# Small loads and norm roots issued earlier, and one placement for every buffer of weight parts, in a two-block transformer kernel

## The chip, the cores and the metric

The kernel runs on one core of a Trainium2 chip. The time is the device time of one execution in microseconds (us), and less is better. PE is the matrix engine, DVE the vector engine, ACT the scalar engine, POOL GpSimd, and SP the engine that issues the weight loads.

## The reference, cut to what matters

Two transformer blocks act on x of 256 tokens by 1024, in float32. The first is a hybrid mixer (a convolution of 31 taps beside an attention over selected blocks), a cross-attention to 256 memory rows, and a SwiGLU layer, followed by a norm. The second is a gated and a dilated branch beside each other, and a layer of 16384 experts.

```python
for l in range(DEPTH):                       # first block
    h = rms_norm(x, norm_mix_g[l])
    x = x + hybrid_mixer(h, w_in[l], conv_dw_w[l], ...)   # w_u ... w_gates, conv_pw_w, w_out
    h = rms_norm(x, norm_x_g[l])
    x = x + cross_attention(h, mem, xq_w[l], xkv_w[l], xo_w[l])
    h = rms_norm(x, norm_ffn_g[l])
    x = x + swiglu(h, ffn_in_w[l], ffn_out_w[l])
x = rms_norm(x, final_norm_g)
h = rms_norm_2(x, norm1_g[layer])            # second block; two norms stand in a row here
proj = h @ w_in[layer]                       # w_uv_2, w_qkv_2
...
x = x + mix @ w_out[layer]                   # w_out_2
x = x + peer(rms_norm_2(x, norm2_g[layer]), w_query[layer], sub_keys[layer], expert_u[layer], expert_v[layer])
```

## The kernel before, in words

**Products in three parts.** A float32 product is made from parts: a weight is cast to a shorter float (hi), the rest is a second one (lo), and the activations are held as hi and lo as well (hh and hl). A product is hi·hh + hi·hl + lo·hh. `form2` (L273) holds the weight still and streams 256 tokens past it: a unit of half a chunk is 24 matmuls. `form1` (L283 to L285) holds the activations still and streams 512 weight columns.

**The stream of weights.** `Stream` loads chunks of 1 MB through SP into three raw buffers, in the order of use. Each chunk is two units. ACT casts a unit to hi (L100), DVE subtracts to lo (L111); hi and lo go into pairs of buffers used in turn, four of them at first, six where `add_pairs` has added hi_x and lo_x. In pair 0 the parts of some weights (the tuple `moved`) begin 40 elements further on. DVE's subtraction frees the raw buffer, and so lets SP issue the next chunk. ACT and DVE take their work strictly in the order of the program: a part that stands behind a waiting instruction waits too.

**Late work.** `defer` and `pending` hold an evacuation back until some matmuls of the next unit stand ahead of it (`run_late`); `bg` is a list of pieces that `run_bg` spreads over the units of a product. `cols2` makes two units and one evacuation, `rows_c` (a product with its result in rows of tokens) ends in `tail`.

**A tail.** `tail` makes the last four chunks of a product in four groups (two halves of tokens, tt, by two of columns, hf), evacuates each (adds the residual, multiplies with the gain of the next norm), squares on ACT, and turns the result with PE (`transpose_split`, L394 or L396) into hh (ACT cast, L400) and hl (DVE, L401), the inputs of the next product. The factor of the norm, 1/root of the mean square, is found per token: an addition on DVE, a power on POOL (L440, L477), then a multiplication into a unit matrix on DVE (`diag`, L442, L483) which PE turns into a row (L484). `scaled_norm` applies the row at the evacuation of the next product, so that the product itself can start without it. `root` calls it from the tail, where the diagonal takes part in the turn.

**Five places.** The change touches the following, in the order of time. Place 0: the convolution's taps (`cacc`, a first tap on ACT at L573, the rest on DVE at L576), which run beside the product w_u. They need the taps' weights `dww` and `cvec`, loaded by POOL at L553 and L556, behind the loads that lay out the position bias: brow is copied to `b_dram` in eight pieces (L544) and read back in two (L547). Place A: the tail of conv_pw_w. Place B: the tail of w_out, with the products xq_w and xkv_k behind it. Place C: the tail of xo_w, with ffn_in_w behind it. Place D: the tail of ffn_out_w, where `after4` makes both norms that stand in a row, with w_uv_2 behind it. Place E: the tail of w_out_2, with w_query_2 behind it.

```python
        st.split(st.n_used + st.ahead)      # tail, before: all splits that have a buffer
        st.flush()
        if after is not None:               # the roots stand behind them
            after(0)
            after(1)
```

## Time and profile before

| what | value |
|---|---|
| median of 3 runs | 1567.42 us (1566.62 to 1567.6) |
| the profiled execution | 1564.88 us, span 1563.1 us |
| PE busy | 1498.3 us, 96% of the span, 9934 matmuls |
| DVE busy | 1124.2 us, 72% |
| ACT busy | 825.9 us, 53% |
| POOL busy | 45.0 us, 3% |
| granted clock, mean | 0.986 |

The span is the time from the first to the last instruction of the trace. The profiled execution is 1.78 us longer than its span and 2.5 us shorter than the median. A busy share is a mean over all stages of the kernel. A granted clock of 1.00 is full speed (2.4 GHz), 0.50 is the lower of the two levels (1.2 GHz).

### The profile page before, as it was taken

What the parts mean: (1) busy time and instruction counts of PE and PEld (TensorE: products, weight loads), DVE (VectorE), ACT (ScalarE), POOL (GpSimd) and SP (SyncE); (2) the same over time, 40 slices, a digit from 0 to 9 for tenths busy, and PEclk for the clock granted to TensorE, in tenths of its full rate; (3) what the DMA queues carried; (4) which work ended last, traced back from release to release, by engine and by line L of the source; (5) the groups of instructions that cost most, each with busy time, mean ns of one, the idle gap of its engine ahead of it and who ended that gap; (6) DMA issues with size and microseconds to landing.
All of it is one profiled execution on the core that took longest, in us unless ns stands there. A gap on an engine that the chain in (4) does not pass through costs nothing.

```text
span 1563.1 us, 25016 instructions
## 1 busy us (share of the span) xinstructions
PE 1498.3 (96%) x9934; PEld 1357.6 (87%) x9934; DVE 1124.2 (72%) x2081; ACT 825.9 (53%) x1316; POOL 45.0 (3%) x86
## 2 busy tenths in 40 slices
PE   7699999997999999799999999999999999999998
PEld 7699788777889988587999999999999888888886
DVE  5597899665567755575889978999996555555555
ACT  5343576744455543564554557776655444444443
POOL 2210000000000000200000000000000000000000
PEclk9899999998999999899999999999999999999999
DMA  8655222454355554541545553343335655555552
GB/s 293 217 202 181 82 82 101 147 197 167 117 189 189 194 210 140 205 156 73 196 166 186 188 190 135 138 156 139 136 136 216 238 202 192 189 191 192 200 197 81
DMA packets 39733, 265.99 MB, mean 170 GB/s; under 512 B 4768, under 2 KB 5072, under 8 KB 9536
## 3 DMA queue, kind: packets, MB, share of 16 engines
q1 hardware_dynamic: 34992, 248.72, 44.1%
q0 software_dynamic: 3616, 12.53, 2.6%
q10 hardware_dynamic: 1008, 3.15, 0.6%
q8 instruction: 78, 1.28, 0.3%
q14 instruction: 39, 0.32, 0.1%
HBM read 258.09 MB, written 5.24 MB: 168 GB/s over the span
## 4 chain that ended last, share of the span: by engine, by line
PE 87%; DVE 5%; DMA 3%; ACT 2%; issue 1%; POOL 1%; SPq 0%; POOLq 0%; ACTq 0%; DVEq 0%
PE mm L273 36%; PE mm L285 12%; PE mm L284 12%; PE mm L283 12%; PE tp L1481 4%; DVE lo L111 2%; PE tp L263 2%; PE tp L273 2%; DMA b_dram<-brow 1%; DVE cacc L576 1%; PE tp L794 1%; PE pv L829 1%; DMA gain<-in_norm_mix_g_dram 1%; PE tp L816 1%; PE tp L394 0%
## 5 line engine op out<-in xcount | busy, mean ns | idle before, releaser
L100 ACT CAST hi<-raw 128x1024 fp32r<-128x1024 f32 x427 | 446.0, 1049 | 441.5 <-PE mm L285 220.8
L111 DVE TENSOR_TENSOR lo<-raw,hi 128x1024 fp32r<-128x1024 f32 x427 | 516.7, 1221 | 91.9 <-ACT hi L100 91.4
L273 PE MATMUL mm<-xnt,hi 128*128 128x256 f32 x2416 | 425.4, 280 | 8.6 <-ACT hi L100 8.6
L273 PEld LDWEIGHTS mm<-xnt,hi 128*128 128x128 f32 x2416 | 367.9, 189 | 9.2 <-ACT hi L100 8.6
L273 PE MATMUL mm<-xnt,lo 128*128 128x256 f32 x1208 | 336.4, 278 | 0.5 <-DVE lo L111 0.5
L273 PEld LDWEIGHTS mm<-xnt,lo 128*128 128x128 f32 x1208 | 228.5, 189 | 0.8 <-DVE lo L111 0.8
L283 PE MATMUL mm<-hi,wring 128*128 128x512 f32 x512 | 199.3, 389 | 1.2 <-ACT wring L256 1.2
L284 PE MATMUL mm<-lo,wring 128*128 128x512 f32 x512 | 199.3, 389 | 0.1
L285 PE MATMUL mm<-hi,wring 128*128 128x512 f32 x512 | 199.3, 389 | 0.1
L273 PE MATMUL mm<-hh,hi 128*128 128x256 f32 x976 | 172.0, 280 | 3.2 <-DVE hh L401 2.4
L273 PEld LDWEIGHTS mm<-hh,hi 128*128 128x128 f32 x976 | 149.7, 190 | 4.9 <-DVE hh L401 3.0
L273 PE MATMUL mm<-hh,lo 128*128 128x256 f32 x488 | 136.8, 280 | 15.2 <-DVE lo L111 15.2
L257 DVE TENSOR_TENSOR wring<-act,wring 128x512 fp32r<-128x512 f32 x64 | 44.2, 694 | 123.9 <-ACT wring L256 123.9
L283 PEld LDWEIGHTS mm<-hi,wring 128*128 128x128 f32 x512 | 96.1, 188 | 21.4 <-ACT wring L256 1.4
L285 PEld LDWEIGHTS mm<-hi,wring 128*128 128x128 f32 x512 | 96.1, 188 | 20.5 <-DVE wring L257 0.5
L284 PEld LDWEIGHTS mm<-lo,wring 128*128 128x128 f32 x512 | 96.1, 188 | 20.3 <-DVE lo L111 0.6
L576 DVE SCALAR_TENSOR_TENSOR cacc<-vpad,dww,cacc 128x256 f32<-128x256 f32 x240 | 101.0, 485 | 16.4 <-ACT cacc L573 16.4
L273 PEld LDWEIGHTS mm<-hh,lo 128*128 128x128 f32 x488 | 93.1, 191 | 15.6 <-DVE lo L111 15.6
L1487 DVE TENSOR_TENSOR act<-act,tp 128x208 f32<-128x208 f32 (+31 forms) x64 | 57.4, 915 | 10.6 <-PE tp L1481 8.3
L100 ACT CAST hi_x<-raw 128x1024 fp32r<-128x1024 f32 x40 | 41.9, 1051 | 38.6 <-PE mm L273 16.0
L1481 PE MATMUL tp<-raw 128*128 128x128 f32 x512 | 62.2, 275 | 0.0
L1481 PEld LDWEIGHTS tp<-raw 128*128 128x128 f32 x512 | 59.7, 191 | 0.0
(401 smaller groups left out, 2204.8 us busy)
## 6 DMA issues: line engine op xcount, KB each, us to landing
raw<-in_expert_u_dram SPq DMA_DIRECT2D x64, 1024.0 KB, 4.8
raw<-in_expert_v_dram SPq DMA_DIRECT2D x64, 1024.0 KB, 4.8
raw<-in_ffn_in_w_dram SPq DMA_DIRECT2D x22, 1024.0 KB, 4.8
raw<-in_ffn_out_w_dram SPq DMA_DIRECT2D x11, 1024.0 KB, 4.8
raw<-in_w_u_dram SPq DMA_DIRECT2D x8, 1024.0 KB, 8.7
raw<-in_w_g_dram SPq DMA_DIRECT2D x8, 1024.0 KB, 4.8
raw<-in_w_out_dram SPq DMA_DIRECT2D x8, 1024.0 KB, 4.8
raw<-in_w_query_dram SPq DMA_DIRECT2D x8, 1024.0 KB, 5.4
```

Of the source, the lines that this page charges most:

```text
L100: self.nc.scalar.copy(out=hi, in_=raw)
L111: self.nc.vector.tensor_tensor(out=lo, in0=raw, in1=hi.bitcast(F32), op=ALU.subtract)
L257: V.tensor_tensor(out=lo, in0=src, in1=hi.bitcast(F32), op=ALU.subtract)
L263: T.matmul(out=ps, lhsT=a, rhs=b, start=(k == 0), stop=(k == n - 1))
L273: T.matmul(out=ps, lhsT=a[:, k, :], rhs=b[:, k, :], start=k == 0 and n == 0, stop=k == KK - 1 and n == 2)
L283: T.matmul(out=ps, lhsT=a, rhs=r, start=first and k == 0, stop=False)
L284: T.matmul(out=ps, lhsT=a, rhs=q, start=False, stop=False)
L285: T.matmul(out=ps, lhsT=b, rhs=r, start=False, stop=last and k == nk - 1)
L576: V.scalar_tensor_tensor(out=cacc[:, j, :], in0=vpad[:, j, w:w + S], scalar=dww[:, j, w:w + 1], in1=cacc[:, j, :], op0=ALU.mult, op1=ALU.add)
L794: T.matmul(out=sv, lhsT=qT[:, (g // 2) * 4 + r, tt * P:(tt + 1) * P], rhs=ksw[:, g // 2, g % 2, :, 0:n], start=True, stop=True)
L1481: T.matmul(out=ps[:, j * P:(j + 1) * P], lhsT=ring[:, b % 2, 0, j, :], rhs=ring[:, b % 2, 1, j, :], start=True, stop=True)
L1487: V.tensor_tensor(out=o[:, :, 0:there], in0=o[:, :, 0:there], in1=pv[:, :, 0:there], op=ALU.mult)
```

## The change

The loads of small tables at place 0 move ahead of the position bias, and are issued by POOL right behind the first norm's powers. In `tail` the splits that were made at the end move behind the roots, and the units' last split in the middle goes; with a `root` all four groups are now made before the turns. `scaled_norm` makes both diagonals in `after`, right behind the roots, and the row only when an evacuation asks for it. The products of xkv_k that stood between w_out's tail and its last turn come half before it and half behind it. The first products of ffn_in_w and w_query_2 are made in halves: the first four row blocks of both units, then the last four, so that the second half of hh and hl is wanted later. The last turn of conv_pw_w's result is held back into w_out (`hold`), and in `rows_c` run at the third unit. `after4` is gone: its squares, multiplications and roots are spread over the units of w_uv_2 through `bg`, and the first block's final gain is loaded anew by POOL, 512 KB in broadcast, into the tile `ug`, behind the eight loads of that stage. All four pairs of buffers now have one size and begin at one position, and w_v, xkv_v and w_g begin 48 elements further on in every pair. Small spacing tiles, one buffer of `sn` and the place of `skT` follow from that.

```diff
-    def __init__(self, nc, raws, pairs, chunks, plain, ahead, moved):
+    def __init__(self, nc, raws, pairs, chunks, plain, gap, behind):
...
-                at = self.at if pair is self.wide and name in self.moved else 0
+                at = self.gap if name in self.behind else 0
...
-    his, los = ([const.tile([P, HF + 64], F32R, name=f"{n}0")] + fixed(const, 3, F32R, n + "_") for n in ("hi", "lo"))
+    his, los = ([const.tile([P, HF + 64], F32R, name=f"{n}{k}") for k in range(4)] for n in ("hi", "lo"))
...
-    st = Stream(nc, raws, list(zip(his, los)), chunks, ("mem", "cmp_w1"), AHEAD,
-                ("xkv_k", "w_u", "w_k", "w_c", "w_q", "w_gates", "xq_w", "ffn_in_w", "w_query_2", "expert_u_2"))
+    st = Stream(nc, raws, list(zip(his, los)), chunks, ("mem", "cmp_w1"), GAP, ("w_v", "xkv_v", "w_g"))
...
-    def cols2(name, ah, al, evac, ahead=None):
+    def cols2(name, ah, al, evac, ahead=None, halves=False):
         ps = mm_tile()
+        if halves:
+            pss = [ps[:, 0:S], mm_tile()[:, 0:S]]
+            ws = [st.next(name, st.ahead - m) for m in range(2)]
+            for k in range(0, KK, KK // 2):
+                for m in range(2):
+                    form2(pss[m], ws[m], ah, al, range(k, k + KK // 2))
+                    run_late()
+            st.defer(lambda: evac(*pss))
+            yield
+            yield
+            return
...
+        st.low(st.n_high)
         for hf in range(2):
             prod(0, hf, 0, 4)
             evac(0, hf, pp[0][hf])
         if root is not None:
             root(0)
+            for hf in range(2):
+                prod(1, hf, 0, 4)
+                evac(1, hf, pp[1][hf])
+            root(1)
+            turn(0, (0, 4))
             turn(1, (0,))
+        else:
+            prod(1, 0, 0, 4)
+            evac(1, 0, pp[1][0])
+            turn(0, (0, 4))
+            prod(1, 1, 0, 2)
             turn(1, (0,))
+            prod(1, 1, 2, 4)
+            evac(1, 1, pp[1][1])
         if mid is not None:
-            mid()
+            drive(mid)
         if hold:
             pending.append(lambda: turn(1, (4,)))
         else:
             turn(1, (4,))
-        st.split(st.n_used + st.ahead)
-        st.flush()
         if after is not None:
             after(0)
             after(1)
+        while mid is not None and drive(mid):
+            pass
+        st.split(st.n_used + st.ahead)
+        st.flush()
...
         for c in range(n - 4):
             w = st.next(name)
+            if c == 2:
+                run_late()
...
         def after(tt):
...
+            dg[tt] = wk.tile([P, P], F32, tag="diag", name="diag")
+            V.tensor_scalar(out=dg[tt], in0=ident, scalar1=r, scalar2=32.0, op0=ALU.mult, op1=ALU.mult)
...
-    rows_c("w_out", 4, yh, yl, **ends, mid=lambda: all_of(mem_keys(3, 0)))
-    rrow = row(1.0 / 16)
+    rows_c("w_out", 4, yh, yl, **ends, mid=mem_keys(3, 0))
+    x_row = row
...
-        all_of(cols2("ffn_in_w", hh, hl, ffn_evac(j)))
+        all_of(cols2("ffn_in_w", hh, hl, ffn_evac(j), halves=j == 0))
...
-    rows_c("ffn_out_w", DFF // 256, fh, fl_, evac=evac4, after=after4, hold=True,
+    rows_c("ffn_out_w", DFF // 256, fh, fl_, evac=evac4, hold=True,
...
+    g_f, junk = (t.rearrange("p t d -> p (t d)") for t in (ug, aout))
+    nc.gpsimd.dma_start(out=g_f, in_=I["final_norm_g"].partition_broadcast(P))
+
+    def squares(n):
+        for tt in range(2):
+            A.activation(out=junk, in_=x[:, tt, :], func=ACTF.Square, accum_out=ssq[tt][:, n:n + 1])
+
+    def gained():
+        for tt in range(2):
+            V.tensor_tensor(out=x[:, tt, :], in0=x[:, tt, :], in1=g_f, op=ALU.mult)
...
+    bg.extend((1.0, f) for f in (lambda: squares(0), gained, lambda: squares(1), roots, scaled))
...
-    all_of(cols1("w_uv_2", hh, hl, v_evac))
-    all_of(cols1("w_uv_2", hh, hl, u_evac))
+    all_of(cols1("w_uv_2", hh, hl, v_evac), 1.0)
+    all_of(cols1("w_uv_2", hh, hl, u_evac), 1.0)
```

What follows are pieces of each engine's instruction list, in its order. The first is POOL's at place 0: the powers of the first norm (rs), the table loads, and the bias rows.

```order
-L544 DMA b_dram<-brow 16x16x384 x8
-L547 DMA bias<-b_dram 128x8x256 x2
-L551 MEMSET vpad 128x8x30
-L553 DMA dww<-in_conv_dw_w_dram 128x248
-L556 DMA cvec<-in_conv_dw_b_dram 128x8
...
+L554 DMA dww<-in_conv_dw_w_dram 128x248
+L557 DMA cvec<-in_conv_dw_b_dram 128x8
...
+L567 MEMSET ones_c 128x128
+L568 MEMSET cbias 128x512
+L582 DMA b_dram<-brow 16x16x384 x8
+L585 DMA bias<-b_dram 128x8x256 x2
```

The eight small loads stand ahead of the copies of brow now; the copies and the reads of bias come last.

The second is DVE's at place B, the end of w_out's tail; xnl is hl there, mm a product's result, lo and lo_x are parts of weights. First the kernel before, then the changed one.

```order
L469 TENSOR_TENSOR x<-x,mm 128x512
L470 TENSOR_TENSOR xg<-x,gain 128x512
L401 TENSOR_TENSOR xnl<-tp,xnh 128x4x128
L111 TENSOR_TENSOR lo_x_3076<-raw_82,hi_x_3074 128x1024
L111 TENSOR_TENSOR lo_80<-raw_82,hi_76 128x1024
L111 TENSOR_TENSOR lo_81<-raw_83,hi_77 128x1024
L111 TENSOR_TENSOR lo_78<-raw_83,hi_74 128x1024
L111 TENSOR_TENSOR lo_79<-raw_84,hi_75 128x1024
L476 TENSOR_SCALAR rs_3317<-ss_3171 128x1
L476 TENSOR_SCALAR rs_3320<-ss_3204 128x1
L483 TENSOR_SCALAR diag<-ident,rs_3317 128x128
L483 TENSOR_SCALAR diag<-ident,rs_3320 128x128
```

```order
L487 TENSOR_TENSOR x<-x,mm 128x512
L488 TENSOR_TENSOR xg<-x,gain 128x512
L418 TENSOR_TENSOR xnl<-tp,xnh 128x4x128
L494 TENSOR_SCALAR rs_3281<-ss_3174 128x1
L497 TENSOR_SCALAR diag<-ident,rs_3281 128x128
L494 TENSOR_SCALAR rs_3286<-ss_3207 128x1
L497 TENSOR_SCALAR diag<-ident,rs_3286 128x128
L111 TENSOR_TENSOR lo_x_3070<-raw_82,hi_x_3068 128x1024
L111 TENSOR_TENSOR lo_80<-raw_82,hi_76 128x1024
L111 TENSOR_TENSOR lo_81<-raw_83,hi_77 128x1024
L111 TENSOR_TENSOR lo_78<-raw_83,hi_74 128x1024
```

The two roots and diagonals, which stood behind five subtractions, stand ahead of them.

The third is DVE's at place D, behind the last evacuation of ffn_out_w; xnt is hl there, ug the gain, x the stream of rows. First the kernel before, from its first final multiplication on, then the changed one.

```order
L111 TENSOR_TENSOR lo_81<-raw_83,hi_77 128x1024
L1111 TENSOR_TENSOR x<-x,gain 128x1024
L1113 SCALAR_TENSOR_TENSOR rs_5570<-ssq 128x1
...
L1118 TENSOR_SCALAR x<-x,ssq 128x1024
L111 TENSOR_TENSOR lo_78<-raw_83,hi_74 128x1024
L111 TENSOR_TENSOR lo_79<-raw_84,hi_75 128x1024
L401 TENSOR_TENSOR xnt<-tp,xnt 128x4x128
```

```order
L111 TENSOR_TENSOR lo_81<-raw_83,hi_77 128x1024
L111 TENSOR_TENSOR lo_78<-raw_83,hi_74 128x1024
L1166 TENSOR_TENSOR x<-x,ug 128x1024 x2
L111 TENSOR_TENSOR lo_79<-raw_84,hi_75 128x1024
L418 TENSOR_TENSOR xnt<-tp,xnt 128x4x128
L111 TENSOR_TENSOR lo_x_3069<-raw_84,hi_x_3067 128x1024
L1170 SCALAR_TENSOR_TENSOR rr_5603<-ssq_5601 128x1
```

Of the two chains of multiplication, root and scaling only the two multiplications, which now read ug, are left ahead of xnt; the subtraction lo_78 has moved ahead of them.

## Rows read from the trace of the kernel before

**Rows 1.** The page's first part: busy time, share, instructions.
```profile
PE 1498.3 (96%) x9934; PEld 1357.6 (87%) x9934; DVE 1124.2 (72%) x2081; ACT 825.9 (53%) x1316; POOL 45.0 (3%) x86
```
**Rows 2.** What PE waited for: us in total, times, longest.
```profile
PE mm L273 <- DVE lo L111: 15.6, 3, 14.5
...
PE tp L484 <- DVE diag L483: 8.6, 1, 8.6
```
**Rows 3.** Place 0, timelines: start, duration, instruction, [idle before <- releaser].
```profile
23.87 4.51 POOL L544 DMA_DIRECT2D b_dram<-brow  x8 [3.36 <-DVE brow L538]
...
53.38 0.54 POOL L556 DMA_DIRECT2D cvec<-in_conv_dw_b_dram  x1
...
44.78 1.05 ACT L100 CAST hi<-raw 128x1024 fp32r<-128x1024 f32 x1 [1.46 <-DMA raw<-in_w_u_dram]
60.55 1.09 ACT L573 ACTIVATE cacc<-vpad,cvec,dww 128x256 f32<-128x256 f32 x2 [14.72 <-DMA cvec<-in_conv_dw_b_dram]
...
61.18 2.13 DVE L576 SCALAR_TENSOR_TENSOR cacc<-vpad,dww,cacc 128x256 f32<-128x256 f32 x4 [16.35 <-ACT cacc L573]
...
64.50 0.58 PE L273 MATMUL mm<-hh,lo 128*128 128x256 f32 x1 [14.53 <-DVE lo L111]
```
**Rows 4.** Windows: PE, PEld, DVE, ACT, POOL busy (instructions), granted clock, DMA share, GB/s.
```profile
75.00:85.00 10.00, 10.00 (x90) 10.00 (x89) 10.00 (x19) 4.04 (x6) 0.00 (x0) 1.00 0.48 190
367.20:371.70 4.50, 4.48 (x21) 4.50 (x22) 1.51 (x2) 1.31 (x2) 0.06 (x1) 0.50 0.47 193
632.00:640.00 8.00, 3.67 (x8) 2.47 (x9) 5.20 (x9) 3.53 (x5) 7.15 (x12) 0.50 0.54 177
```
**Rows 5.** Place A, timeline of PE.
```profile
328.47 0.63 PE L394 MATMUL tp<-ident,y 128*128 128x128 f32 x4 [2.11 <-DVE y L942]
```
**Rows 6.** Place B, timeline of DVE.
```profile
361.36 4.63 DVE L111 TENSOR_TENSOR lo<-raw,hi 128x1024 fp32r<-128x1024 f32 x4
...
366.79 0.28 DVE L483 TENSOR_SCALAR diag<-ident,rs 128x128 f32<-128x128 f32 x1 [0.57 <-POOL rs L477]
...
375.53 0.69 DVE L981 TENSOR_TENSOR xq<-tp,rrow 128x512 f32<-128x512 f32 x1 [4.49 <-PE tp L273]
```
**Rows 7.** Place C, timeline of PE.
```profile
442.40 0.68 PE L484 MATMUL tp<-diag,ones 128*128 128x128 f32 x4
```
**Rows 8.** Place D, timelines of DVE, PE and POOL.
```profile
619.70 0.68 DVE L1103 TENSOR_TENSOR x<-x,mm 128x512 f32<-128x512 f32 x1
...
624.43 1.22 DVE L1111 TENSOR_TENSOR x<-x,gain 128x1024 f32<-128x1024 f32 x1
...
633.86 0.89 POOL L1130 DMA_DIRECT2D rope<-in_c_rope_dram  x1
...
637.55 0.79 PE L285 MATMUL mm<-hi_x,xnt 128*128 128x512 f32 x1 [1.09 <-DVE xnt L401]
...
638.49 1.95 POOL L1143 MEMSET dk<- 64x1024 f32 x2
```
**Rows 9.** DMA issues from 625 to 662 us: KB each, median us to landing.
```profile
wsT<-in_w_spatial_dram POOLq DMA_DIRECT2D x1, 512.0 KB, 4.9
...
gv<-in_out_norm_b_g_dram POOLq DMA_DIRECT2D x1, 256.0 KB, 9.6
```
**Rows 10.** Place E, timeline of PE.
```profile
739.59 3.06 PE L396 MATMUL tp<-diag,xg 128*128 128x128 f32 x16 [2.88 <-DVE diag L442]
```
**Rows 11.** Two units of ffn_in_w, timeline of PE: the matmuls on lo.
```profile
448.63 0.28 PE L273 MATMUL mm<-hh,lo 128*128 128x256 f32 x1
...
451.01 0.28 PE L273 MATMUL mm<-hh,lo 128*128 128x256 f32 x1
...
453.81 0.28 PE L273 MATMUL mm<-hh,lo 128*128 128x256 f32 x1
```
**Rows 12.** One line's instructions: ns shortest, median, longest; first and last start.
```profile
L273 PE MATMUL mm<-xnt,hi x2416: 276/276/682, 8.6 to 1205.1; 128*128 128x256 f32 x186
...
L273 PE MATMUL mm<-hh,hi x976: 274/276/579, 26.9 to 554.8; 128*128 128x256 f32 x196
```

More of the change, by code (lines that the diff above doesn't have):

```diff
@@ L38 @@
 class Stream:
-    def __init__(self, nc, raws, pairs, chunks, plain, ahead, moved):
+    def __init__(self, nc, raws, pairs, chunks, plain, gap, behind):
         self.nc, self.free, self.pairs, self.chunks = nc, list(raws), pairs, chunks
-        self.wide, self.at, self.moved = pairs[0], ahead, moved
+        self.gap, self.behind = gap, behind
         self.units = []
@@ L409, in x_tile @@
         return res.tile([P, 2, D], F32, tag="x", name="x")
+    par.tile([P, 16], F32, name="gap")
     st.load(2)
@@ L530, in tile_model @@
     drive(key_steps[0])
-    drive(key_steps[1])
-    b_ps = tp_tile()
-    T.matmul(out=b_ps[:, 0:LB], lhsT=rb, rhs=oneh, start=True, stop=True)
-    V.tensor_tensor(out=brow, in0=b_ps[:, 0:LB], in1=brow, op=ALU.add)
-    turn(0)
-    drive(key_steps[1])
-    turn(1)
-    b_dram = tc.dram_tile([16, P, LB], F32, name="b_dram")
-    for r in range(8):
-        nc.gpsimd.dma_start(out=b_dram[:, 16 * r:16 * r + 16, :], in_=bc(brow[16 * r:16 * r + 16, :].unsqueeze(1), [16, 16, LB]))
-    b_ap = b_dram[:, :, :]
-    for n in range(2):
-        nc.gpsimd.dma_start(out=bias[:, 8 * n:8 * n + 8, :],
-                            in_=bass.AP(tensor=b_ap.tensor, offset=b_ap.offset + n * 8 * P * LB + P - 1,
-                                        ap=[[LB - 1, P], [P * LB, 8], [1, S]]))
     vpad = m1.tile([P, KK, CW - 1 + S], F32, tag="vpad", name="vpad")
@@ L567, in tile_model @@
     nc.gpsimd.memset(cbias, NEG)
+    drive(key_steps[1])
+    b_ps = tp_tile()
+    T.matmul(out=b_ps[:, 0:LB], lhsT=rb, rhs=oneh, start=True, stop=True)
+    V.tensor_tensor(out=brow, in0=b_ps[:, 0:LB], in1=brow, op=ALU.add)
+    turn(0)
+    drive(key_steps[1])
+    turn(1)
+    b_dram = tc.dram_tile([16, P, LB], F32, name="b_dram")
+    for r in range(8):
+        nc.gpsimd.dma_start(out=b_dram[:, 16 * r:16 * r + 16, :], in_=bc(brow[16 * r:16 * r + 16, :].unsqueeze(1), [16, 16, LB]))
+    b_ap = b_dram[:, :, :]
+    for n in range(2):
+        nc.gpsimd.dma_start(out=bias[:, 8 * n:8 * n + 8, :],
+                            in_=bass.AP(tensor=b_ap.tensor, offset=b_ap.offset + n * 8 * P * LB + P - 1,
+                                        ap=[[LB - 1, P], [P * LB, 8], [1, S]]))
     cacc = m1.tile([P, KK, S], F32, tag="cacc", name="cacc")
@@ L1090, in tile_model @@
         gains_2(j)
-        all_of(cols2("ffn_in_w", hh, hl, ffn_evac(j)))
+        all_of(cols2("ffn_in_w", hh, hl, ffn_evac(j), halves=j == 0))
     xg = res.tile([P, 2, D], F32, tag="xv", name="xg")
     hh, hl = parts_of(xnt_p, "xnt", False)
-    r2 = [par.tile([P, 2], F32, name=f"r2_{tt}") for tt in range(2)]
     def evac4(tt, hf, ps):
@@ L1325, in tile_model @@
     peer = ctx.enter_context(tc.tile_pool(name="peer", bufs=1))
-    skT = peer.tile([P, 2, P], F32, name="skT")
-    nc.gpsimd.dma_start(out=skT, in_=I["sub_keys_2"])
     iota_f = peer.tile([P, P], F32, name="iota_f")
@@ L1335, in tile_model @@
     scr2 = act[:, 64:96, :].rearrange("p i t -> p (i t)")
+    skT = scr2[:, 2816:3072].rearrange("p (a k) -> p a k", a=2)
+    nc.gpsimd.dma_start(out=skT, in_=I["sub_keys_2"])
     def flat(lo, n):
@@ L1371, in query_evac, with evac @@
     def query_evac(h):
[L1372 to L1374 removed]
+        def evac(*pss):
+            qts[h], n = scr2[:, 6144 + (h % 2) * 512:6144 + (h % 2 + 1) * 512], 512 // len(pss)
+            for m, ps in enumerate(pss):
+                A.copy(out=qts[h][:, n * m:n * m + n], in_=ps)
         return evac
@@ L1391, in tile_model @@
     for h in range(8):
-        for n, _ in enumerate(cols2("w_query_2", xh, xl, query_evac(h))):
+        for n, _ in enumerate(cols2("w_query_2", xh, xl, query_evac(h), halves=h == 0)):
             if n == 0 and h > 0:
```

95 lines of the change are left out of this document (41 added, 54 removed).

## The prediction

> **What bounds the kernel now.** The page's first part says that PE is busy for 96% of the span [rows 1]: what can be won is either idle time of PE, about 65 us, or time per matmul. So I read next what PE waited for. Two of the waits there are single and long: 14.5 us for a subtraction lo, 8.6 us for a diagonal [rows 2]. The timelines of each engine around these places, and around the other tails, show who was late: a table of the convolution, roots behind weight splits, a last half of hl. Last I compared matmuls of the buffers of weight parts, since the change moves every pair. In the rows the reader is to see, for each wait, the instruction in front of it on the engine that was late.
>
> **Place 0, small loads.** PE stops until lo ends and goes on at 64.50. That lo stands on DVE behind four taps of 2.13 us, which begin at 61.18 after a wait of 16.35, for ACT's first tap at 60.55, which waited 14.72 us for cvec. POOL issued cvec only at 53.38, behind the eight copies of brow that began at 23.87 and the reads of bias that waited for them [rows 3]. In the change cvec is issued some 2 us after POOL's powers, between 21 and 26 us, and the copies of brow start about eight issues of 0.54 us later less the 3.36 us that POOL waited for brow, so 2 us later. The landing has 20 us. What ends last is then ACT's cast of 44.78 + 1.05 = 45.8; the first tap follows at once instead of at 60.55: 14.7 us earlier. PE waited 14.5 [rows 3]. Is the gain kept? From 75 to 85 us DVE is busy 10.00 of 10 us [rows 4]; this stretch is paced by DVE's taps, so the whole chain moves forward with its start. The one thing that could take it back is the supply of weights, because ACT waited 1.46 us for a raw buffer at 44.78 [rows 3]; the reads of bias and the small tables share the transfers. I take **14.6**, with 11 (weights 3.5 us late) and 16 (also the matmuls at half the clock behind the wait) as bounds.
>
> **Place A.** PE waited 2.1 us for y before the turn at 328.47 [rows 5]. The turn is held back into the next product, but the splits now stand behind the evacuations of y, so that the first lo of w_out is ready about when PE comes to it. The wait changes its name: **0**, from -0.5 to +2.
>
> **Place B.** Behind w_out's tail DVE made four subtractions of 4.63 us from 361.36 and only then the roots; the diagonal came at 366.79, PE had waited 8.6 us for it, and xq was evacuated at 375.53 [rows 2, 6]. Now both roots and diagonals stand ahead of the splits, and the row is asked for only after 48 matmuls of xq_w. Those wait for one lo_x, until 360.8 (by its place behind the hl of the turn; the row's four subtractions begin at 361.36, which bounds it). 48 matmuls at 0.113 us [rows 11] end at 366.2, two turns of the diagonal later 366.7, against about 375.3 before. The stretch from 367.2 to 371.7, at a granted clock of 0.50 [rows 4], is in it. **8.7**, with 7 and 10.5 as bounds (the serial chain of add, power, diagonal: 0.57 us of waiting and 0.28 in the row, twice).
>
> **Place C.** Before, two units and the diagonal end at 442.40 + 0.44 [rows 7]. The halves let both units begin with what hl there is; but the second half waits for an ACT cast that stands behind two splits now, and for DVE behind the roots. Counting these I reach 441.9: **1**, from -0.5 to +2.
>
> **Place D.** Before, POOL had the roots' powers in its queue and could issue rope only at 633.86; PE had the last part of xnt at 637.55 [rows 8]. The two multiplications (1.22 us each), roots and scalings no longer stand ahead. But they are not free: both multiplications still stand ahead of lo_79 and of the last xnt on DVE, and they now wait for `ug`. POOL is free for the stage's loads when ffn_out_w's last matmul is done, at 619.7. Eight issues take 4.6 us (633.86 to 638.49), the memset 1.95 [rows 8]: ug is issued near 626.3. When does it land? A load of 512 KB took 4.9 us, the last of the eight, 256 KB behind the others and beside the weights, 9.6 [rows 9]: between 631.2 and 635.9. Two chunks of weights are under way as well; I take 6.2 us, 632.5. Behind it stand 2 x 1.22 + 1.16 + 0.69 = 4.3 us on DVE: PE goes on at 636.8 instead of 637.55, **0.7** earlier, from +2 to -2.7 by these two rows. So the wait for roots becomes a wait for a transfer, and the half clock from 632 to 640 [rows 4] stays. The Trainium skill (DMA: Bandwidth & Descriptors, section on the anatomy of one DMA) fits a POOL load as 2.0 us and bytes at 436 GB/s, by which an estimate for ug is 3.2 us and the sum would be 3.0 better; its section "Issuing engines are not separate DMA queues" says that loads of all engines share the same 16 DMA engines, which speaks against that.
>
> **Place E.** The wait of 2.88 us for the diagonal at 739.59 [rows 10] goes, since the groups are made before the turns and the halves delay the need for the last hl. Two small waits for lo and hl replace it, 0.9 and 0.5 us: **2**, from 0.5 to 2.5.
>
> **Pairs of parts.** Three matmuls of one unit take 0.340 us ((451.01 - 448.63) / 7), in the next 0.350 (2.80 / 8) [rows 11]: 113.3 and 116.7 ns. The slow one is in pair 0, whose parts began 40 elements on. With six pairs one unit in six is slow, with four one in four. By the program some 55 units of 24 matmuls lie in pair 0 under a moved name: 55 x 24 x 3.3 ns = 4.4 us, 0.4 of it in the stretch that DVE paces. For w_v, xkv_v and w_g, 298 matmuls of 512 columns, the position changes too; no row compares them, so by twice the columns 0 to 2 us, taken as 1. **5.0**, if the new common position is the fast one; 0 if it isn't the position that costs, 7 if the waits behind other matmuls go as well. The Trainium skill speaks against this term (TensorE: Matmul & The Clock Gate, section "Step-by-step: what each phase is for"): PE has two independent ports to read SBUF, so a load of weights doesn't take bandwidth from the matmul that runs. By it the positions could not matter and the sum would be 5.0 smaller; the pitch of 0.350 beside 0.340 is not explained by it.
>
> The smaller buffers of sn, the loads of skT and the spacing tiles: 0. sn's third buffer covered DVE, which runs ahead of PE there; if that cover went, a softmax row would wait for one exponential, well under 1 us.
>
> **Sum.** 14.6 + 0 + 8.7 + 1 + 0.7 + 2 + 5.0 = 32.0 us, made against the profiled execution: 1564.88 - 32.0 = 1532.9. That run is 2.5 us under the median of the runs shown, so the median comes to 1567.42 - 32.0 = **1535.4**.
>
> **Rivals.**
> (1) The pairs give nothing: 27 us are left, 1540.4. For it speaks that only pair 0 is seen slow and that any position other than its own may do; against it that pairs 1 to 3 were uniform and fast, and the new ones are alike.
> (2) ug lands late, behind the weights (9.6 us or more) [rows 9], and the halves at C and E give nothing because their inputs are late as well: 32.0 - 3.4 - 1.5 - 1.5 = 25.6, so 1541.8. The two can meet: 1547.
> (3) The gains are larger: ug lands after 4.9 us, place A's turn costs nothing any more, the waits behind other matmuls go with the pairs, and B and 0 reach their upper bounds: 1.3 + 2 + 2 + 1.8 + 1.4 = 8.5 more, 1526.9.
> (4) Slower: the common position is the slow one for every pair. There are 1.5 x (2416 + 976) = 5088 matmuls with xnt and hh [rows 12]. The other terms give 27, so that it decides from 27 / 5088 = 5.3 ns per matmul on; at 5.9 the kernel takes 1570.4. The largest excess in the rows is 3.4 ns [rows 11], which makes 17 us and 1557.7 instead: still faster.
> (5) The change does not do what it says at place 0: the small loads stall behind the weights, which fill the transfers then, and cvec lands as late as before. 14.6 us are lost: 1550. Against it speaks the slack of 20 us.
>
> **How the numbers follow.** My forecast, with the spread of its terms, has 0.66; rival 1 0.12, 2 0.08, 3 0.07, 5 0.04, 4 0.03. The range reaches to rival 3's time and to rivals 1 and 2 together, less what two in ten may leave out: 1526 to 1546. What a measurement of this kernel can tell from no change is about 0.2%, 3 us. Every case but the extreme of rival 4 lies below that: faster 0.96, same 0.02, slower 0.02.
>
> **What would show it.** In the changed profile: at place 0 the first cacc on ACT near 46, PE without the wait of 14.5 us and DVE full from there on; at B no wait for a diagonal, the evacuation of xq about 9 us earlier; at D a wait of PE of some 10 us for xnt, with the multiplication on ug as DVE's waiting instruction, released by the transfer; at E a wait under 1 us; all units at 0.340 us for three matmuls, also the one in six. The prediction is wrong where weights become the wait at place 0, where PE's pitch stays mixed, or where ug's wait exceeds 13 us.

## The result and the profile after

Four runs of the changed kernel took 1549.69 us (median; 1548.74 to 1551.78), four of the kernel before beside them 1567.51 (1566.62 to 1568.14). The ratio is 0.9889 with an interval of 0.9871 to 0.9906: 17.8 us less, within some 15 to 20. That is faster, but 14.3 us above the forecast of 1535.4 and 3.7 above the end of its range.

The profiled executions lie 14.6 us apart (spans 1563.1 and 1548.5, at a mean granted clock of 0.986 and 0.993); the ledger below adds up to that. The page of the changed kernel, first part (busy time, share, instructions):

```profile
PE 1501.0 (97%) x9934; PEld 1358.2 (88%) x9934; DVE 1124.8 (73%) x2082; ACT 826.1 (53%) x1317; POOL 45.8 (3%) x87
```

PE has the same 9934 matmuls as in [rows 1], yet is busy for 1501.0 us instead of 1498.3. So matmuls became no cheaper, and on the whole all that was won is idle time. The waits of PE after the change (us in total, times, longest):

```profile
PE mm L282 <- DVE xnt L418: 11.9, 1, 11.9
PE mm L270 <- ACT hi L100: 8.4, 1, 8.4
...
PE mm L281 <- DVE lo L111: 2.7, 2, 1.9
...
PE tp L270 <- DVE lo_x L111: 1.8, 1, 1.8
...
PE tp L413 <- DVE diag L460: 1.1, 1, 1.1
```

The 14.5 us of place 0 and the 8.6 us of place B [rows 2] are gone (at B the forecast wait for one lo_x takes its place, 1.8 us), and the diagonal of place E costs 1.1 instead of 2.88 [rows 10]. The second line is the start of the program, which the change leaves alone. The first, at place D, is new and the longest of all.

**Where the time went.** The two traces hold the same matmuls. I paired them and took, at the borders of each place, the start after less the start before; the difference between two borders is what that stretch gained.

| stretch (us, before) | predicted | measured |
|---|---|---|
| place 0, 49 to 112 | -14.6 | -12.2 |
| w_u and on, 112 to 322 | | -0.8 |
| place A, 322 to 332 | 0 | +1.3 |
| w_out, 332 to 350, with A's last turn | | +0.4 |
| place B, 350 to 376 | -8.7 | -8.6 |
| place C, 428 to 446 | -1 | +0.5 |
| ffn_in, 446 to 560 | part of -5.0 | +3.8 |
| place D, 625 to 650 | -0.7 | +2.05 |
| place E, 720 to 752 | -2 | -1.5 |
| expert layer, 752 to 1220 | part of -5.0 | +0.8 |

These rows make -14.25; the stretches between them, and 0.2 ahead of 49 us, hold the other 0.3. This is one execution of each kernel: in the eleven other profiles with small loads moved ahead (below), place 0 alone comes to between -12.0 and -14.7.

**Place 0 after**, timelines of ACT, DVE and PE:

```profile
47.06 1.05 ACT L100 CAST hi<-raw 128x1024 fp32r<-128x1024 f32 x1 [7.14 <-DMA raw<-in_w_u_dram]
48.02 1.09 ACT L593 ACTIVATE cacc<-vpad,cvec,dww 128x256 f32<-128x256 f32 x2
...
48.65 1.77 DVE L596 SCALAR_TENSOR_TENSOR cacc<-vpad,dww,cacc 128x256 f32<-128x256 f32 x4 [7.41 <-ACT cacc L593]
...
51.61 0.38 PE L270 MATMUL mm<-hh,lo 128*128 128x256 f32 x1 [1.84 <-DVE lo L111]
```

DVE's chain starts at 48.65 instead of 61.18 [rows 3], 12.5 us earlier, and that is kept, as the stretch is paced by DVE (10.00 of 10 us busy from 75 to 85, as before). The first tap doesn't wait for `cvec`; it stands behind a cast that waits for a weight chunk, now 7.14 us and not 1.46, and ends at 48.11 where I took 45.8.

**Place A after**, PE and DVE, and the windows behind (busy time of PE, PEld, DVE, ACT and POOL, granted clock, DMA share, GB/s):

```profile
314.53 3.49 DVE L111 TENSOR_TENSOR lo<-raw,hi 128x1024 fp32r<-128x1024 f32 x3
...
315.81 0.50 PE L281 MATMUL mm<-lo,hh 128*128 128x512 f32 x1 [1.92 <-DVE lo L111]
```

```profile
317.00:320.40 3.40, 3.40 (x10) 2.65 (x9) 1.02 (x1) 0.00 (x0) 0.00 (x0) 0.50 0.95 340
```

The wait for y (2.11, [rows 5]) became a wait of 1.92 for lo, as predicted. What I left out follows: ten matmuls at half the clock, 3.40 us where 1.70 would do. In the profile of before, the clock stood at 1.00 there. But this stretch doesn't belong to the new tail alone. The same window of the kernel "Small loads alone" below, which has the old tail and the old wait of 2.1 for y, and then of "Pair 0 as before", which has the new tail and a wait of 1.91 for lo:

```profile
316.00:319.40 3.40, 3.40 (x10) 2.62 (x9) 2.48 (x3) 3.35 (x5) 0.97 (x2) 0.50 0.67 152
```

```profile
317.90:321.30 3.40, 3.40 (x16) 2.81 (x15) 0.98 (x1) 0.00 (x0) 0.00 (x0) 1.00 0.91 337
```

So behind a stop of some 2 us at this place the half clock came in some of these profiles and not in others.

**Place C after**, the windows where ffn_in_w begins, in the changed kernel and in "The gain first" below:

```profile
419.40:422.80 3.40, 3.40 (x19) 3.40 (x18) 1.24 (x2) 1.28 (x2) 0.00 (x0) 0.50 0.64 236
```

```profile
419.40:422.80 3.40, 3.40 (x32) 3.40 (x31) 1.52 (x3) 2.57 (x4) 0.00 (x0) 1.00 0.66 181
```

PE's waits at this place are the same in both (1.7, 0.7 and 0.4 us), and both have the pairs alike. The first executes 19 matmuls in the stretch, the second 32. This half clock is what turns place C from a gain of 1.1 into a loss of 0.5: of the eleven profiles with the changed tail, the two that have it lose 0.5 and the nine others gain 1.1.

**Place D after**, POOL, DVE and PE, and two rows of DMA issues (KB each, us to landing):

```profile
603.51 0.61 POOL L1134 DMA_DIRECT2D rope<-in_c_rope_dram  x1 [187.28 <-PE mm L282]
...
609.78 0.54 POOL L1158 DMA_DIRECT2D ug<-in_final_norm_g_dram  x1
...
619.35 2.36 DVE L1166 TENSOR_TENSOR x<-x,ug 128x1024 f32<-128x1024 f32 x2 [10.14 <-DMA ug<-in_final_norm_g_dram]
...
623.50 0.80 PE L282 MATMUL mm<-hi_x,xnt 128*128 128x512 f32 x1 [11.87 <-DVE xnt L418]
```

```profile
raw<-in_w_qkv_dram SPq DMA_DIRECT2D x3, 1024.0 KB, 7.8
...
ug<-in_final_norm_g_dram POOLq DMA_DIRECT2D x1, 512.0 KB, 9.5
```

From POOL's release to the issue of ug are 6.3 us (6.6 forecast), from its landing to PE 4.15 (4.3 forecast); the landing itself took 9.5 and not 6.2.

**The pitch after.** Matmuls on lo of one unit of ffn_in; two rows are eight steps of three matmuls apart:

```profile
428.30 0.28 PE L270 MATMUL mm<-hh,lo 128*128 128x256 f32 x1
...
431.12 0.28 PE L270 MATMUL mm<-hh,lo 128*128 128x256 f32 x1
```

2.82 / 8 = 0.353 us, 117.5 ns for a matmul (117.7 over a whole unit), and it is so in every unit of ffn_in. Before, it was 113.3, with 116.7 in pair 0 [rows 11]. All buffers now have one position, but not one pitch: the durations of single matmuls (0.28) show none of it, only their distances do.

### The profile page after: what moved, and what is told of

Its sections match the earlier page's. It is cut to its first block, busy times and chain, and to the rows that moved or that the text cites. A ratio compares the mean times of both kernels' runs of the same rounds, so it can differ in the third digit from the quotient of the medians.

```text
span 1548.5 us, 25023 instructions
## 1 busy us (share of the span) xinstructions
PE 1501.0 (97%) x9934; PEld 1358.2 (88%) x9934; DVE 1124.8 (73%) x2082; ACT 826.1 (53%) x1317; POOL 45.8 (3%) x87
## 4 chain that ended last, share of the span: by engine, by line
PE 68%; DVE 2%; ACT 1%; issue 1%; DMA 1%; POOL 1%; POOLq 0%; ACTq 0%; DVEq 0%
PE mm L270 32%; PE mm L282 10%; PE mm L280 10%; PE mm L281 10%; PE tp L1517 4%; DVE lo L111 1%; DMA ug<-in_final_norm_g_dram 1%; PE tp L1419 0%; PE tp L1278 0%; PE pv L262 0%; ACT hi L100 0%; PE tp L1292 0%; PE tp L411 0%; ACT dk L1254 0%; DVE act L1470 0%
## 5 line engine op out<-in xcount | busy, mean ns | idle before, releaser
L111 DVE TENSOR_TENSOR lo_x<-raw,hi_x 128x1024 fp32r<-128x1024 f32 x40 | 48.5, 1221 | 16.0 <-ACT hi_x L100 15.6
```

The source lines that it names most:

```text
L111: self.nc.vector.tensor_tensor(out=lo, in0=raw, in1=hi.bitcast(F32), op=ALU.subtract)
```

## The experiments

Each kernel was timed in four runs (the sixth in ten) beside the kernel before on the same chip, whose medians were 1567.23 to 1568.12; edits are to the changed kernel unless said otherwise. Three questions were open: what made ffn_in longer, what the new waits at A and D cost, and what kept place 0 from its 14.6. My theory on the first: PE has two pitches at the common position and stays in the one it is in; a unit at another position brings it back to the short one, which pair 0 had been doing by accident. The rival: the pitch belongs to the position alone.

**Pair 0 as before.**

```diff
-                at = self.gap if name in self.behind else 0
+                at = self.gap if name in self.behind else 40 if pair[0].shape[1] > HF and pair is self.wide and name in MOVED else 0
```

> The changed kernel, with pair 0 again 40 elements on for the ten weights that had it before; all else as changed. Theory 1 (one odd pair resets PE): all pairs alike leave nothing that brings PE out of its slower pitch once it is in it. Expects ffn_in_w back to 0.340 us for three matmuls in five units of six and 0.350 in the one in pair 0 (the changed kernel shows 0.353 in all), 3 to 4 us saved there, about 1 us more at the end of expert_u_2, some 1 us lost where the changed kernel is at 0.340 throughout; sum 2.5 to 4 us faster than the changed kernel, about 1546. Theory 2 (the position costs by itself, as in my prediction): every unit in pair 0 gets slower and nothing else changes: about 4 us slower, 1554.

1543.09 us (1542.49 to 1544.67), ratio 0.9847 [0.983, 0.9863]: 6.6 less than the changed kernel. The trace shows the turn, in matmuls of PE on lo in ffn_in:

```profile
426.09 0.28 PE L272 MATMUL mm<-hh,lo 128*128 128x256 f32 x1
...
428.92 0.28 PE L272 MATMUL mm<-hh,lo 128*128 128x256 f32 x1
...
432.42 0.28 PE L272 MATMUL mm<-hh,lo 128*128 128x256 f32 x1
...
434.46 0.28 PE L272 MATMUL mm<-hh,lo 128*128 128x256 f32 x1
```

The first two rows, at the common position, are 2.83 / 8 = 0.353 apart. Between 429.27 and 432 runs a unit of pair 0, at 0.350. Behind it, at the common position again, six steps take 2.04: 0.340. From there to the end of ffn_in, and again through the expert layer, the matmuls lie where those of before lay, less a constant. Against the changed kernel's profile ffn_in gives 3.6 of the 5.6 us between the two, the expert layer 0.8. Not the pitch's doing are 1.5 at place A and 1.6 at place C, where this kernel shows no half clock: kernels below with alike pairs gain 1.1 at place C too. The granted clock is 0.994 to 0.995 in its four runs and 0.992 to 0.993 in those of the changed kernel, about 3 us of time. The rest goes the other way.

**One unit only.** The same for the first ffn_in unit in pair 0 alone.

```diff
+                if name == "ffn_in_w" and pair is self.wide and not self.shifted:
+                    at = self.shifted = 40
```

> The changed kernel with one unit of ffn_in_w alone, the first that falls to pair 0, placed 40 elements on; all other units as changed. Theory 1 (reset): the units behind it run at 0.340 us for three matmuls until something disturbs them, so most of the 3.8 us that ffn_in_w lost comes back: 2.5 to 3.8 us faster than the changed kernel, about 1546.5. Theory 2 (each unit has its own pitch by its position and nothing is remembered): only this one unit changes, by less than 0.1 us: 1549.7.

1544.72 (1543.48 to 1546.87), 0.9856 [0.9839, 0.9872]. Matmuls on lo, of the long pitch ahead of the shifted unit and behind it:

```profile
426.50 0.28 PE L272 MATMUL mm<-hh,lo 128*128 128x256 f32 x1
...
428.98 0.28 PE L272 MATMUL mm<-hh,lo 128*128 128x256 f32 x1
...
432.48 0.28 PE L272 MATMUL mm<-hh,lo 128*128 128x256 f32 x1
...
434.52 0.28 PE L272 MATMUL mm<-hh,lo 128*128 128x256 f32 x1
```

2.48 / 7 = 0.354 ahead of it, 2.04 / 6 = 0.340 behind it. One shifted unit of 24 matmuls brought the rest of ffn_in to 113.3 ns, where the five profiles without a shifted unit have 117.7 throughout. In w_query and the expert layer, without a shifted unit, this execution ran at 117.7 up to 860 us, where the changed kernel's was at the short pitch: against before, 3.1 us lost there and 0.7 gained in the changed kernel. So both pitches exist at one position, and the rival falls.

**The gain first.** `ug` is issued ahead of the eight other loads of the stage, and the memset behind them.

```diff
-    nc.gpsimd.dma_start(out=rope, in_=I["c_rope"])
+    loads = [(rope, I["c_rope"])]
...
+    for o, i in loads:
+        nc.gpsimd.dma_start(out=o, in_=i)
+    for e in range(2):
+        nc.gpsimd.memset(dk[64 * (1 - e):64 * (1 - e) + 64, :, e], 0.0)
...
```

> The changed kernel with the load of the first block's final gain (ug) issued first of its stage, ahead of the eight other loads and the memset. Theory 1 (the wait at w_uv_2 is that transfer, issued 6.3 us late and queued behind 1.9 MB of its own queue and three chunks of weights): ug is issued near 603.5, lands near 607.5 and DVE multiplies from about 609.2; the wait of 11.9 us shrinks to about 2, the half clock with it: 9 to 11 us faster than the changed kernel, about 1539.5. Rival (the squares on ACT and the roots are what is late, the load only comes last by a little): 0 to 3 us, 1547 or more.

1536.96 (1532.94 to 1539.65), 0.98 [0.9783, 0.9817]: 12.7 less. POOL, DVE and PE at place D, and the window of ten us behind POOL's release:

```profile
602.04 0.60 POOL L1156 DMA_DIRECT2D ug<-in_final_norm_g_dram  x1 [185.71 <-PE mm L282]
...
607.65 2.35 DVE L1168 TENSOR_TENSOR x<-x,ug 128x1024 f32<-128x1024 f32 x2
...
611.80 0.50 PE L282 MATMUL mm<-hi_x,xnt 128*128 128x512 f32 x1 [1.64 <-DVE xnt L418]
```

```profile
602.00:612.00 10.00, 7.95 (x36) 5.97 (x35) 9.97 (x11) 9.55 (x14) 6.78 (x11) 1.00 0.82 276
```

The landing took 4.2 us; DVE doesn't wait, as its splits end later than that. PE waits 1.64 instead of 11.87, and the clock stays at 1.00. Place D then gains 10.1 against before, instead of losing 2.05: the order of one load is worth 12.1, of which 10.2 is the wait; the rest is about what the half clock cost behind it in the changed kernel, where PE was busy for 4.10 us from 623.0 to 627.6 at a granted clock of 0.50. From POOL's release the issue comes 6.3 us earlier than in the changed kernel, and the landing is 5.3 shorter.

**Split early.** In the tail of conv_pw_w one split is made ahead of the last evacuations.

```diff
             prod(1, 1, 0, 2)
+            if early:
+                st.split(max(st.n_high, st.n_used + 1))
             turn(1, (0,))
...
```

> The changed kernel, but in conv_pw_w's tail the split of the next unit is made again ahead of the last evacuation, as before. Theory 1 (the moved split made the new wait of 1.9 us for lo at the first unit of w_out, and the half clock of 3.3 us behind it): both go, 3 to 4.5 us faster than the changed kernel, about 1546. Rival (the wait only moves: PE then waits for the evacuation of y, as it did before, or for hh): 0 to 1 us, 1549.

1543.93 (1542.98 to 1546.8), 0.9851 [0.9835, 0.9868]: 5.8 less. DVE at place A:

```profile
310.55 1.23 DVE L111 TENSOR_TENSOR lo<-raw,hi 128x1024 fp32r<-128x1024 f32 x1
...
312.29 0.68 DVE L963 TENSOR_TENSOR y<-y,mm 128x512 f32<-128x512 f32 x1
```

The subtraction stands ahead of the evacuation, PE has no wait for lo at w_out's first units, and place A goes from +1.3 to -2.7. That is 4.0 less, 1.7 of it the half clock, and all six profiles with this edit show -2.7 and no half clock there. The rest of the 5.8 is not settled: the two profiles lie 3.5 apart, with 1.3 more ahead of 112 us and 1.6 at place C, and 1.2 at place E and 2.3 in the expert layer the other way, none of it touched by the edit.

**Two small loads instead of all.** Only `dww` and the first part of `cvec` go ahead; the other tables are issued behind the bias again.

```diff
-    for n, nm in enumerate(("conv_dw_b", "conv_ln_g", "conv_ln_b")):
-        nc.gpsimd.dma_start(out=cvec[:, n, :], in_=I[nm])
+    nc.gpsimd.dma_start(out=cvec[:, 0, :], in_=I["conv_dw_b"])
...
```

> The changed kernel, but of the eight small loads only dww and the first cvec stay ahead of the bias rows; the other six go behind them again. Theory 1 (the traffic of the small tables, put into a stretch in which the transfers are full, made the weights of w_u 2.3 us later, and these now set the start of the taps: ACT's cast at 47.06 instead of 44.78): the first cacc starts near 46.5 instead of 48.02, PE's wait of 2.1 us at 49.5 falls below 1, 1 to 2 us faster than the changed kernel by this stretch. Rival (the copies of brow that start and end later, or the weights alone, set it; the six loads do not matter): the first cacc at 48 as before, no change. Between executions the pitch of PE can add or take 2 us, so that the stretch up to 112 us of the timeline is what decides.

1547.64 (1546.89 to 1549.58), 0.9874 [0.9857, 0.989]; the interval overlaps that of the changed kernel. In the trace ACT's cast begins at 46.18 instead of 47.06, PE has no wait for lo behind it, and place 0 gains 14.0 instead of 12.2. But that is no more than executions differ by: in the ten profiles of kernels with all eight loads ahead the cast begins between 45.74 and 47.78 and place 0 gains 12.0 to 14.7; four of the ten casts are earlier than this one. That the six tables delay the chunk is not shown.

**The pairs alone.** The kernel before, with nothing but the new positions, the smaller sn and the moved skT.

```diff
-                at = self.at if pair is self.wide and name in self.moved else 0
+                at = self.at if name in self.moved else 0
...
+                ("w_v", "xkv_v", "w_g"))
```

> The kernel before with nothing but the change's pairs of buffers (all alike, w_v, xkv_v and w_g 48 elements on in each), and the smaller buffer of sn and the place of skT that make room for them. My prediction's term: 5.0 us faster than before, 1562.5. Theory 1 (pair 0 was what brought PE out of its slower pitch): ffn_in_w runs at 0.353 us for three matmuls, or at 0.340 in all units if PE happens to enter it in the fast pitch; the other stages likewise, one way or the other for a whole stage. Expects 0 to 7 us slower than before, 1567 to 1574, with runs further apart than before's.

1567.01 (1564.17 to 1571.17, ten runs) against 1567.28 (1565.61 to 1569.43, thirteen): 1.000 [0.9991, 1.001]. The part that I had put at 5.0 us gives nothing on average. Its runs lie 7.0 us apart, those of before 3.8. The profiled execution is the longest of the ten, 1571.17, and its ffn_in has the long pitch, 2.83 for eight steps:

```profile
447.64 0.28 PE L273 MATMUL mm<-hh,lo 128*128 128x256 f32 x1
...
450.47 0.28 PE L273 MATMUL mm<-hh,lo 128*128 128x256 f32 x1
```

All five profiles of kernels with the pairs alike (the changed kernel, this one, "The gain first", "Split early" and "Two small loads") have ffn_in at the long pitch, and each takes 3.8 us more there than before. In w_query and the first part of the expert layer they differ: two are at the long pitch, 3.1 us slower than before from 752 to 860, three at the short one, 0.7 faster. With one profile of each kernel it stays open whether that is the kernel or the execution, and whether the ten runs differ by the same cause. Nor is it settled why the pairs cost nothing on average here, while bringing pair 0 back into the changed kernel gave 6.6, about 3 of it by the clock.

**The three repairs together:** pair 0 as before, the gain first, the split early.

> The changed kernel with the three corrections together: pair 0 again 40 elements on, ug loaded first, the split ahead of the last evacuation in conv_pw_w's tail. If the three causes are separate, their gains of 6.6, 12.7 and 5.8 us add up, less what the pitch gave by chance in two of them: 1524 to 1529. If two of them shared a cause (the half clock, or the pitch after a wait), 1530 or more.

1528.59 (1527.24 to 1531.6), 0.976 [0.9744, 0.9777]: 21.1 less than the changed kernel. The three gains add up to 25.1; in the profiles each of the three holds place C's 1.6, and two of them the half clock at place A, which can be had once only. The page's first part:

```profile
PE 1491.7 (98%) x9934; PEld 1350.1 (89%) x9934; DVE 1123.8 (74%) x2082; ACT 826.1 (54%) x1317; POOL 45.9 (3%) x87
```

Now PE is busy for less than before the change as well.

**One shifted pass in four.** The three repairs, with pair 0 shifted in every fourth turn of the buffers only.

```diff
+                at = self.gap if name in self.behind else 40 if pair is self.wide and name in MOVED and self.n_high // len(self.pairs) % 4 == 0 else 0
```

> As the kernel with the three corrections, but pair 0 is 40 elements on in one pass over the pairs in four only. Theory 1 (one odd unit resets PE, and the fast pitch then lasts until something disturbs it): the units of pair 0 in the other passes run at 0.340 too, 1 to 3 us faster than with every pass. Rival (each pass needs its own reset, the fast pitch does not last by itself): units at 0.353 between the odd ones, 2 to 5 us slower.

1531.44 (1529.6 to 1532.36), 0.9774 [0.9758, 0.979]; the interval doesn't part it from the kernel with all repairs, and its profile was 2.3 us longer. Matmuls of ffn_in on lo:

```profile
456.94 0.28 PE L272 MATMUL mm<-hh,lo 128*128 128x256 f32 x1
...
459.41 0.28 PE L272 MATMUL mm<-hh,lo 128*128 128x256 f32 x1
...
462.92 0.28 PE L272 MATMUL mm<-hh,lo 128*128 128x256 f32 x1
...
464.95 0.28 PE L272 MATMUL mm<-hh,lo 128*128 128x256 f32 x1
```

2.47 for seven steps, 0.353, as in all units of ffn_in up to there; then one shifted unit; behind it 2.03 for six, 0.338, with no other matmul between. The way back is shown again. In the expert layer the long pitch set in behind four other matmuls at 840.04 and lasted up to 883. There a shifted unit and four other matmuls stood before the short pitch, so that either can have ended it. The hoped-for gain from fewer shifted units isn't shown: a disturbance now costs up to four turns of the buffers.

**Both again, with two loads.** The three repairs and the two small loads.

> The kernel with the three corrections (pair 0, ug first, split early), and of the eight small loads only dww and the first cvec ahead of the bias rows. If the traffic of the other six is what delays the weights of w_u, the 0.9 to 1.7 us that the same edit gave the changed kernel add to the three: 1526.5 to 1528. Rival (the stage is paced by DVE anyway and the gain is lost behind it): 1528.6 as without it.

1530.22 (1527.26 to 1531.36), 0.9764 [0.9745, 0.9782]: no gain over the three repairs. The cast begins at 46.28, and place 0 gains 14.2, again within what the kernels with all eight loads show.

**All pairs shifted.** Gain first, split early, and all four large pairs 40 elements on.

```diff
+                at = self.gap if name in self.behind else 40 if pair[0].shape[1] > HF and name in MOVED else 0
```

> The kernel with ug first and the split early, and all four pairs 40 elements on for the ten weights (hi_x and lo_x stay where they are, so ffn_in_w is mixed). Theory 2, as in my fourth rival (the position itself costs 3.4 ns per matmul): all units of w_query_2 and expert_u_2 at 0.350 us or more for three matmuls, some 10 to 13 us slower than the kernel with the three corrections, 1540. Theory 1 (the position does not cost, a change of position between two units does, and it also resets the pitch): alike pairs run at 0.340 or 0.353 for whole stretches, never at 0.350: 1527 to 1535.

1537.06 (1535.49 to 1537.97), 0.9812 [0.9796, 0.9829], 8.5 more than the three repairs. In w_query and the expert layer every unit has one pitch:

```profile
784.37 0.28 PE L272 MATMUL mm<-xnt,lo 128*128 128x256 f32 x1
...
787.17 0.28 PE L272 MATMUL mm<-xnt,lo 128*128 128x256 f32 x1
```

2.80 / 8 = 0.350, 116.7 ns, and it returns to it right behind a disturbance. The theory that the shifted position costs nothing of itself falls: it costs 3.3 ns a matmul, as the prediction read it. But it has one pitch, where the common position has two.

**Small loads alone.** The kernel before, with only the small tables issued ahead.

> The kernel before with nothing but the small loads ahead of the bias rows. The prediction's first term gave 14.6 us; the changed kernel's timeline shows 12.4 in that stretch. If the term is separate from all others: 12 to 13 us faster than before, 1555, and the timeline behind it the same as before's but for that shift. Rival (later stages take part of it back, since their weights or the bias rows arrive later): under 10 us, 1558 or more.

1553.26 (1551.89 to 1554.65), 0.9913 [0.9896, 0.9929]: 14.1 less than before. ACT and DVE at place 0:

```profile
46.39 1.05 ACT L100 CAST hi<-raw 128x1024 fp32r<-128x1024 f32 x1 [5.21 <-DMA raw<-in_w_u_dram]
47.34 1.09 ACT L574 ACTIVATE cacc<-vpad,cvec,dww 128x256 f32<-128x256 f32 x2
...
47.97 1.77 DVE L577 SCALAR_TENSOR_TENSOR cacc<-vpad,dww,cacc 128x256 f32<-128x256 f32 x4 [5.49 <-ACT cacc L574]
```

Here too the cast waits for its chunk, and the chain starts 13.2 us earlier. So this one part is most of the whole result: by the medians, each good to some 2.6 us, 14.1 of 17.8, and all the others together give 3.7.

**Four places.** Gain first, split early, and the four pairs at 0, 16, 32 and 48 elements.

```diff
+        self.steps = {id(p): 16 * k for k, p in enumerate(pairs)}
...
+                at = self.gap if name in self.behind else self.steps.get(id(pair), 0) if name in MOVED else 0
```

> The kernel with ug first and the split early, with pairs 0 to 3 at 0, 16, 32 and 48 elements on for the ten weights: four positions beside each other in one kernel. If only the position decides a unit's pitch, each pair has a pitch of its own that comes back in every pass: 0.340 or 0.353 us for three matmuls in pair 0, 0.350 in pairs 1 to 3 if every other position is like the one at 40, or 0.340 in some, and then the sum is 1524 to 1536. If it is the step from one position to another that costs, all units, with a step ahead of each, are at 0.350 or more, pair 0 too, and the sum is 1537 or more.

1544.81 (1542.15 to 1547.69), 0.9852 [0.9826, 0.9879]: 16 more than the three repairs. Matmuls on lo, two of its stretches:

```profile
802.17 0.28 PE L273 MATMUL mm<-xnt,lo 128*128 128x256 f32 x1
...
804.21 0.28 PE L273 MATMUL mm<-xnt,lo 128*128 128x256 f32 x1
...
858.66 0.28 PE L273 MATMUL mm<-xnt,lo 128*128 128x256 f32 x1
...
861.14 0.28 PE L273 MATMUL mm<-xnt,lo 128*128 128x256 f32 x1
```

The same pair takes 2.04 / 6 = 0.340 in the first and 2.48 / 7 = 0.354 in the second. That is pair 0, at the common position: 113.3 ns from 779 to 850 us, 117.8 from 859 to 912. The three other pairs keep one pitch through both stretches, some 118.7, 117.8 and 120.0 ns at 16, 32 and 48 elements. So neither expectation is met: the pitch of each pair comes back with every turn of the buffers, as by the first, but the sum is that of the second, because all three other positions cost more than the 116.7 of the one at 40. Nor do steps to these positions end the long pitch of pair 0, though each turn of the buffers has them. A change of position alone is not the way back; a step of 40 elements was, and what of it does it (it is no multiple of 64 bytes, the others are) wasn't tried further.

## Why the prediction was right and wrong

Predicted were 32.0 us; the profiles lie 14.6 apart. The 17.4 that are missing, by step:

**Pairs of parts: 8.4, the step that failed.** Instead of -5.0, the stretches without another term came to +3.4 together. "5.0, if the new common position is the fast one" took each position to have one pitch. The shifted one does cost 3.3 ns a matmul, as the kernel with all pairs shifted shows. But its unit in each turn also led PE out of a longer pitch of the common position, 117.7 ns, of which the rows I had picked show nothing. Without it ffn_in took 3.8 us more, instead of less. The trace of the kernel before holds that pitch, and against rival 1 I had it that pairs 1 to 3 were uniform and fast. Its expert layer, matmuls on lo in units of pairs 1 and 2:

```profile
945.46 0.28 PE L273 MATMUL mm<-xnt,lo 128*128 128x256 f32 x1
...
947.93 0.28 PE L273 MATMUL mm<-xnt,lo 128*128 128x256 f32 x1
...
950.07 0.28 PE L273 MATMUL mm<-xnt,lo 128*128 128x256 f32 x1
...
952.45 0.28 PE L273 MATMUL mm<-xnt,lo 128*128 128x256 f32 x1
```

2.47 / 7 = 0.353 us, then 2.38 / 7 = 0.340. From 942 to 1170 us this comes sixteen times: behind a group of 16 other matmuls (L1481) stands a unit of pair 0, then pair 1 at the long pitch, and behind the next such group pair 2 at the short one. So other matmuls end the long pitch as well, and the shifted unit does not bring the short one back wherever it stands. In ffn_in and the expert layer of the seven profiles with one shifted pair or unit it did so all eleven times that it stood between two units without other matmuls, the first of them at the long pitch.

Of the rivals the first, that the pairs give nothing, comes nearest: on average they gave 0 in the kernel before. The fourth named an excess that the position can have, not that it comes and goes. The Trainium skill (TensorE: Matmul & The Clock Gate, section "Step-by-step: what each phase is for") has independent ports for weights and the moving operand. That positions could then not matter was my inference from it; I had weighed it against this term, and the sum came out as if by it, yet not for its reason: 113.3, 116.7 and 117.7 ns for the same matmul show that where its weights lie, and what ran before, changes the pitch.

**Place D: 2.75, mis-sized.** The mechanism was the one described, a wait for roots that turns into a wait for a transfer. The term was the landing: 9.5 us, at the bound of 9.6 that I had read and not taken, since I placed ug nearer to the earlier 512 KB load than to the last in the queue. It was the last in the queue. By the Trainium skill's section "Issuing engines are not separate DMA queues" (DMA: Bandwidth & Descriptors), loads of all engines interleave on the same DMA engines. The traces agree: 9.5 us behind eight loads and beside three chunks, 4.2 when it was issued first. How much of the 5.3 between them is the loads ahead of it and how much the chunks was not tried apart.

**Place A: 1.7**, with w_out behind it. The wait that takes the place of the one removed was forecast, its size too. What was lost is the half clock behind it, 1.7 us, within the bound of +2. It isn't the change's own: two kernels with the old tail show it as well, and one with the new tail doesn't.

**Place 0: 2.4.** The bound named it, weights late: 2.3 us. The moved small loads did not stall, so rival 5 falls. That they make the chunk late is not shown; with all eight ahead the gain was 12.0 to 14.7 in ten profiles, and this one is near the lower end. Alone, this part gave 14.1.

**Place C: 1.5** is the half clock from 419.4 to 422.8, not the mechanism: without it the place gains 1.1 of the forecast 1, in nine of the eleven profiles with the changed tail. **Place B** (0.1: 8.6 for 8.7) and **place E** (0.5: 1.5 for 2) stand: no diagonal is waited for at B, and at E 1.1 us is left.

The medians lie 17.8 apart and the profiles 14.6, because the profiled execution of before was 2.6 under its median and the one after 0.6 above.

## What to carry to other kernels

Where a load gates an engine that everything waits for, issue it first in its batch: its place in the queue was worth 12.1 us, more than the work that was moved for it. Put the split of the next weights ahead of the evacuations of a tail, and count a short stop of PE with the half clock that can follow it. Before a difference of one or two us at a place is put down to an edit, look whether a stretch at half clock lies there: two of them came and went here between profiles with nearly the same waits there. Before buffers are made alike, compare the distances of matmuls over whole stages, not over two units: a placement that looks costly may be what ends a worse one.

## What the runs showed of the hardware

A matmul of 256 columns that is 0.28 us long in every record follows the next after 113.3, 116.7 or 117.7 ns, by where the weights lie and by what ran before: at one position both 113.3 and 117.7 lasted over whole stages. A unit of 24 matmuls at 40 elements on, directly behind a unit at the longer pitch and with no other matmuls behind it, ended it eleven times in eleven; groups of other matmuls ended it too, and the longer pitch also set in behind such groups, but not behind each. What begins it isn't settled.

A stretch of 3.4 us at a granted clock of 0.50 followed a stop of PE of about 2 us at place A in some kernels' profiles and not in others, with the old tail and with the new.
